# Where attention's blocks stand among the last projection slabs of a two-layer decoder trunk

## The chip, the core and the metric

The kernel runs on one core of a Trainium2 chip. The metric is device time in microseconds (us): the median of several runs of the whole program. The core has five engines that each run their own instructions in order and wait for each other through semaphores: TensorE (PE, matrix products), VectorE (DVE), ScalarE (ACT), GpSimd (POOL) and SyncE (SP, which here only issues transfers).

## What is computed

Two decoder layers over 512 tokens of width 1024. The first mixes with a causal convolution, the second with differential attention; each is followed by a gated feed-forward network and a gated per-layer embedding. The change concerns the attention of the second layer: 8 heads, each with two pairs of queries and keys of width 64 and values of width 128.

```python
qkv = x @ w_qkv
q, k, v = jnp.split(qkv, 3, axis=-1)
q = rms_norm(q.reshape(B, S, N_HEADS, 2, HEAD_DIM), q_g) * (HEAD_DIM ** -0.5)
k = rms_norm(k.reshape(B, S, N_HEADS, 2, HEAD_DIM), k_g)
...
def block(args):          # one block of 128 queries, all heads
    logits = jnp.einsum('bhcqd,bhckd->bhcqk', q_blk, k).astype(jnp.float32)
    logits = logits + bias[None, :, None]
    logits = jnp.where(dist >= 0, logits, -jnp.inf)
    probs = jax.nn.softmax(logits, axis=-1)
    w = probs[:, :, 0] - lam * probs[:, :, 1]
    return jnp.einsum('bhqk,bhkd->bhqd', w.astype(v.dtype), v)
...
o = rms_norm(o, sub_g) * (1.0 - lambda_init)
return o.reshape(B, S, N_HEADS * V_DIM) @ w_o
```

## The kernel before

Every fp32 product is made of three faster ones: a factor is split into a rounded part (`hi`) and the rest (`lo`), and `mm3` (lines 164 to 166) multiplies lo by hi, hi by lo and hi by hi. A weight tile arrives by DMA as `wraw`, ACT rounds it to `whi` (line 157), and DVE, for some tiles POOL, subtracts to get `wlo` (line 159).

**Slabs.** The projection to queries, keys and values is cut into seven slabs, listed in `QKV`. A slab of queries and keys (`"q"`, one pair of heads, 512 columns) takes four weight tiles; the values come as one full slab (`"v", (0, 4)`: heads 0 to 3, 512 columns) and two half slabs of 256 columns and two weight tiles each (heads 4 and 5, heads 6 and 7). Each slab is worked through in four units of 128 tokens (`tb` = 0 to 3), and a unit is 24 matmuls (8 chunks of the width, three products each) into a PSUM tile `mm`.

A unit of queries and keys (`unit`, then `unit_end`) is followed by a chain over the engines: ACT copies and squares (lines 909 and 912), DVE reduces (916), POOL takes the inverse root and scales (229 and 919), PE transposes (925), ACT and DVE write the split queries and keys (933, 934, 941, 943) and POOL copies (938). A unit of values only needs one row on ACT (892) and one on DVE (893).

**Blocks of attention.** Head `hd` and query block `qb` (0 to 3) make one block; its keys are the first 128 (qb + 1), so the four blocks of a head are 128, 256, 384 and 512 wide. A block has three stages. `stage_s`: PE makes the scores of both halves of a head into PSUM tiles `sc` (lines 970 and 971; tiles for up to 256 columns hold both halves), of which there are two; DVE adds the bias and takes the running minimum in one pass (973, called a reduction below), ACT takes the exponential (977), DVE combines both halves (980, 981, 982). `stage_t`: PE transposes the weights (990) into a tile `tp`, ACT and DVE split them (992, 993). `stage_a`: PE multiplies by the values (1006, 1007), and after each second block ACT and DVE collect the result (1013, 1014); after the fourth, lines 1018 to 1028 normalize the head. Blocks follow each other in order of head and query block; the scores of block n are written beside the transposes of block n - 2 and the products of block n - 3.

**What sets the order.** The stages of all blocks stand in one list. The third entry of each slab, its pace, says how many blocks each unit takes from it; a block is three entries, and they are written between the first matmuls of the unit:

```python
for what, at, pace in QKV:
    ws = slab(GLO if what == "q" and at > 0 else 0, P * at[1] if what == "v" else S)
    for tb in range(4):
        between = take(3 * pace[tb])
        between += [None] * (6 - len(between))
        ...
        if what == "v":
            values(at, ws, tb, between)
        else:
            waiting = unit(at, ws, tb, between)
```

What the slabs have not taken is spread over the projections that follow (`step`, inside `project` and the output projection). From the order in which the program is written a scheduler makes each engine's order of instructions; it may bring rows forward or back by a unit or so. The order is fixed in the program; the chip doesn't change it.

Of the kernel before, what the change touches and what calls it, by code (L numbers as in the profile page):

```python
# [64 lines left out]
for _c in range(NC):  # L65
    if _c in PHASED:
        TAPS += [(_c, g, m) for g in range(NPH) for m in (0, 4)] + [(_c, None, LAGS - 1)]
    else:
# [17 lines left out]
STEPS = (2, 2, 2, 3, 4, 5)  # L86
SEVEN = ((0,3),(1,0),(1,1),(1,2),(1,3),(2,0),(2,1),(2,2))
QKV = (("q", 0, (0, 0, 0, 0)), ("v", (0, 4), (0, 1, 1, 0)), ("q", 1, (1, 1, 2, 2)), ("q", 2, (0, 1, 2, 0)), 
       ("v", (4, 2), (1, 1, 1, 1)), ("q", 3, (0, 2, 0, 1)), ("v", (6, 2), (1, 1, 1, 1)))


@with_exitstack
# [1152 lines left out]
```

## Time and profile before

| | |
|---|---|
| median of 3 runs | 1267.42 us (1265.94 to 1268.10) |
| profiled execution | 1268.78 us; its span 1267.0 us |
| PE busy, share of the span | 1244.6 us, 98% |
| DVE busy | 903.4 us, 71% |
| ACT busy | 614.7 us, 49% |
| POOL busy | 263.3 us, 21% |
| mean granted clock of PE | 0.992 |

All times in the profile come from one execution, counted from the start of its span. The engines' busy times overlap, and a busy PE need not be working at its peak: matmuls are pipelined, so that the time from one start to the next is shorter than the duration shown. The granted clock is 1.00 when PE may run at full speed. In the rows of the trace, `out<-in` names the tiles without their numbers, and a bracket at the end gives the idle time of the engine just before the row and the instruction that ended it.

### The profile page before, as it was taken

Reading aid. Unit: us, or ns where it says so; the run is one execution under the profiler, and the core shown is the slowest. Engines: PE = TensorE matmul, PEld = TensorE weight load, DVE = VectorE, ACT = ScalarE, POOL = GpSimd, SP = SyncE. Lnnn points to the kernel's source line nnn. Section 1 sums busy time; section 2 is a strip of 40 time slices with the busy share of each in tenths; the row PEclk is TensorE's granted clock in tenths of the full one; section 3 lists DMA queues with packets and bytes.
Section 4 is the critical chain, followed back from the end, with each engine's and each line's share of the span. In section 5 each row is a group of like instructions: output and inputs, shape, how many; then the busy total and the mean of one; then the engine's idle time right before and its main releaser. Section 6 shows DMA issues by size and latency. Waiting matters only on the chain.

```text
span 1267.0 us, 18622 instructions
## 1 busy us (share of the span) xinstructions
PE 1244.6 (98%) x7152; PEld 1089.2 (86%) x7152; DVE 903.4 (71%) x1482; ACT 614.7 (49%) x1023; POOL 263.3 (21%) x231
## 2 busy tenths in 40 slices
PE   9999899999999999999999999999999999999998
PEld 7888678888899889988888978778898999899887
DVE  6997765975588558667678869845965588558665
ACT  6742464542355335456566757734542355235442
POOL 2852522000000000042516633122000000000030
PEclk9999999999999999999999989999999999999999
DMA  7665123474466444243222214213464467444241
GB/s 296 195 194 178 58 68 115 124 184 124 120 176 180 127 124 121 63 145 100 87 93 75 76 42 123 94 51 115 131 162 138 111 175 188 141 105 117 82 133 67
DMA packets 60597, 158.39 MB, mean 125 GB/s; under 512 B 6451, under 2 KB 11059, under 8 KB 60508
## 3 DMA queue, kind: packets, MB, share of 16 engines
q1 hardware_dynamic: 53776, 136.99, 34.3%
q0 software_dynamic: 4608, 16.78, 8.1%
q10 hardware_dynamic: 2124, 3.43, 0.9%
q8 instruction: 56, 0.92, 0.3%
q14 instruction: 33, 0.27, 0.1%
HBM read 151.91 MB, written 4.21 MB: 123 GB/s over the span
## 4 chain that ended last, share of the span: by engine, by line
PE 87%; DVE 6%; DMA 2%; ACT 2%; issue 1%; POOL 1%; SPq 0%; DVEq 0%; ACTq 0%; POOLq 0%
PE mm L164 24%; PE mm L165 24%; PE mm L166 24%; PE tp L166 2%; PE tp L165 2%; PE tp L164 2%; PE sc L165 1%; PE sc L166 1%; PE sc L164 1%; DVE wlo L159 1%; POOL wk L409 1%; DMA po<-big 1%; PE sc L370 1%; PE mm L1006 1%; DVE sc L421 1%
## 5 line engine op out<-in xcount | busy, mean ns | idle before, releaser
L165 PE MATMUL mm<-A,whi 128*128 128x512 f32 (+1 forms) x904 | 311.8, 346 | 1.0 <-DVE A L569 0.7
L164 PE MATMUL mm<-A,wlo 128*128 128x512 f32 (+1 forms) x904 | 308.0, 345 | 3.5 <-ACT A L178 1.8
L166 PE MATMUL mm<-A,whi 128*128 128x512 f32 (+1 forms) x904 | 310.2, 344 | 0.0
L157 ACT CAST whi<-wraw 128x1024 fp32r<-128x1024 f32 (+2 forms) x150 | 151.1, 1015 | 224.5 <-PE mm L166 98.5
L159 DVE TENSOR_TENSOR wlo<-wraw,whi 128x1024 fp32r<-128x1024 f32 (+2 forms) x147 | 185.1, 1262 | 58.4 <-ACT whi L157 58.1
L164 PEld LDWEIGHTS mm<-A,wlo 128*128 128x128 f32 x904 | 171.4, 190 | 25.0 <-ACT A L178 2.7
L165 PEld LDWEIGHTS mm<-A,whi 128*128 128x128 f32 x904 | 171.9, 190 | 22.1 <-issue 1.2
L166 PEld LDWEIGHTS mm<-A,whi 128*128 128x128 f32 x904 | 171.9, 190 | 21.0 <-issue 1.4
L165 PE MATMUL mm<-B,whi 128*128 128x512 f32 x368 | 143.9, 392 | 0.0
L166 PE MATMUL mm<-B,whi 128*128 128x512 f32 x368 | 143.8, 392 | 0.0
L164 PE MATMUL mm<-B,wlo 128*128 128x512 f32 x368 | 141.6, 393 | 0.0
L675 POOL DMA_DIRECT2D C<-in_wts x32 | 28.1, 880 | 511.8 <-DVE h L786 179.0
L204 POOL TENSOR_TENSOR acc<-acc,wk 128x512 f32<-128x512 f32 x35 | 56.4, 1610 | 218.1 <-ACT wk L203 110.7
L166 PEld LDWEIGHTS mm<-B,whi 128*128 128x128 f32 x368 | 69.5, 189 | 15.0
L166 PE MATMUL mm<-whi,A 128*128 128x512 f32 (+1 forms) x224 | 82.0, 367 | 0.0
L164 PEld LDWEIGHTS mm<-B,wlo 128*128 128x128 f32 x368 | 69.5, 189 | 14.3
L165 PEld LDWEIGHTS mm<-B,whi 128*128 128x128 f32 x368 | 69.4, 189 | 14.3
L165 PE MATMUL mm<-wlo,A 128*128 128x512 f32 (+1 forms) x224 | 81.6, 367 | 0.0
L164 PE MATMUL mm<-whi,A 128*128 128x512 f32 (+1 forms) x224 | 81.6, 370 | 0.0
L786 DVE TENSOR_TENSOR h<-mm,h 128x512 f32<-128x512 f32 x48 | 33.0, 687 | 64.6 <-PE mm L166 64.4
L229 POOL TENSOR_TENSOR r<-v,mhalf 128x8 f32<-128x8 f32 (+1 forms) x31 | 45.4, 1465 | 118.4 <-DVE v L227 93.1
L668 DVE TENSOR_TENSOR wlo<-wraw,whi 128x1024 fp32r<-128x1024 f32 x32 | 39.2, 1224 | 31.5 <-ACT whi L667 31.4
(271 smaller groups left out, 2674.2 us busy)
## 6 DMA issues: line engine op xcount, KB each, us to landing
wraw<-in_wts SPq DMA_DIRECT2D x162, 512.0 KB, 3.6
C<-in_wts SPq DMA_DIRECT2D x32, 512.0 KB, 4.8
C<-in_wts POOLq DMA_DIRECT2D x32, 512.0 KB, 6.1
bias<-in_wts SPq DMA_DIRECT2D x32, 256.0 KB, 3.4
wraw<-in_wts SPq DMA_DIRECT2D x16, 384.0 KB, 3.1
D<-in_diag SPq DMA_DIRECT2D x22, 256.0 KB, 4.5
C<-in_diag SPq DMA_DIRECT2D x16, 256.0 KB, 4.7
h<-in_xT SPq DMA_DIRECT2D x8, 256.0 KB, 5.5
```

Source lines behind the costliest of these rows:

```text
L157: A.copy(hi[:, cut], raw[:, cut])
L159: eng.tensor_tensor(lo[:, cut], raw[:, cut], f(hi[:, cut]), ALU.subtract)
L164: T.matmul(acc, al, bh, start=first, stop=False)
L165: T.matmul(acc, ah, bl, start=False, stop=False)
L166: return T.matmul(acc, ah, bh, start=False, stop=last)
L204: self.last = self.eng.tensor_tensor(self.acc, self.acc, sq, ALU.add)
L229: last_pow[0] = G.tensor_tensor(r[:, :n], v[:, :n], mhalf[:, :n], ALU.pow)
L370: last_tap[0] = T.matmul(acc[:, g * P : (g + 1) * P], w, ups[c][:, g, LEAD - m : LEAD - m + P], start=(m == 0), stop=(m == LAGS - 1),)
L409: G.tensor_tensor(pacc, pacc, pr, ALU.add)
L668: V.tensor_tensor(lo, raw, f(hi), ALU.subtract)
L675: nc.gpsimd.dma_start(q, wts[i + 2].rearrange("p (a s) -> p a s", a=2), accum_op=ALU.add)
L786: V.tensor_tensor(h[m], acc, h[m], ALU.add)
```

## The change

One table of numbers is changed: the paces of the last three slabs. In blocks per unit:

| slab | before | now |
|---|---|---|
| values of heads 4 and 5 (half slab) | 1, 1, 1, 1 | 0, 1, 0, 1 |
| queries and keys of heads 6 and 7 | 0, 2, 0, 1 | 1, 2, 1, 2 |
| values of heads 6 and 7 (half slab) | 1, 1, 1, 1 | 1, 1, 1, 0 |

```diff
 QKV = (("q", 0, (0, 0, 0, 0)), ("v", (0, 4), (0, 1, 1, 0)), ("q", 1, (1, 1, 2, 2)), ("q", 2, (0, 1, 2, 0)), 
-       ("v", (4, 2), (1, 1, 1, 1)), ("q", 3, (0, 2, 0, 1)), ("v", (6, 2), (1, 1, 1, 1)))
+       ("v", (4, 2), (0, 1, 0, 1)), ("q", 3, (1, 2, 1, 2)), ("v", (6, 2), (1, 1, 1, 0)))
```

Both tables take eleven blocks in these three slabs, so that the tail begins with the same block. The list's first entries are shorter (the first blocks have no transposes or products beside them), so the scores are a little ahead of the count. Before, the first half slab wrote the scores of head 3's blocks 1, 2, 3 and head 4's block 0, the slab of queries and keys those of head 4's blocks 1, 2, 3, and the last half slab all four of head 5. Now the first half slab writes head 3's blocks 1 and 2, the slab of queries and keys head 3's block 3, all of head 4 and head 5's block 0, and the last half slab head 5's blocks 1, 2 and 3.

In the rows below a name is a tile with its number; `sc` are scores, `mm` sums of a slab or of the products with the values, `tp` transposes, `C` split queries and keys, `B` values, `A` the normalized input of the projections. Numbers of tiles differ between the programs.

PE, at the end of the half slab of heads 4 and 5, before. `sc_6955` is the second half of head 3's 512-wide block, `sc_7005` is head 4's block 0:

```order
L970 MATMUL sc_6955<-C_1095_6055,C_1093_6053 128x512
L971 MATMUL sc_6955<-C_1097_6057,C_1093_6053 128x512
L990 MATMUL tp_6894<-ident_65,big_6672 128x128
L1007 MATMUL mm_6866<-B_1051_5867,wtl_6826 128x128
L1006 MATMUL mm_6866<-B_1065_5941,wth_6825 128x256
L1007 MATMUL mm_6866<-B_1065_5941,wtl_6826 128x128
L1006 MATMUL mm_6866<-B_1077_5997,wth_6825 128x256
L1007 MATMUL mm_6866<-B_1077_5997,wtl_6826 128x128
L1006 MATMUL mm_6866<-B_1079_6025,wth_6825 128x256
L1007 MATMUL mm_6866<-B_1079_6025,wtl_6826 128x128
L970 MATMUL sc_7005<-C_1191_6465,C_1189_6463 128x128
L971 MATMUL sc_7005<-C_1193_6467,C_1189_6463 128x128
```

Only eight small rows stand between the scores of head 3's last block and those of head 4; the scores of head 4's block 1 (`sc_7130`) come next, and then the slab of queries and keys begins.

PE at the same place now, from the first row of the slab of queries and keys (`mm_7006`) on; `sc_7037` and `sc_7043` are head 3's 512-wide block:

```order
L164 MATMUL mm_7006<-whi_6975,A_928_5273 128x512
L165 MATMUL mm_7006<-wlo_6976,A_927_5272 128x512
L166 MATMUL mm_7006<-whi_6975,A_927_5272 128x512
L990 MATMUL tp_6863<-ident_65,big_6635 128x128 x4
L164 MATMUL mm_7006<-whi_6975,A_931_5283 128x512
L165 MATMUL mm_7006<-wlo_6976,A_930_5282 128x512
L166 MATMUL mm_7006<-whi_6975,A_930_5282 128x512
L970 MATMUL sc_7037<-C_1094_6054,C_1092_6052 128x512
L971 MATMUL sc_7037<-C_1096_6056,C_1092_6052 128x512
L970 MATMUL sc_7043<-C_1095_6055,C_1093_6053 128x512
L971 MATMUL sc_7043<-C_1097_6057,C_1093_6053 128x512
L164 MATMUL mm_7006<-whi_6981,A_939_5326 128x512
```

The scores of head 3's last block now stand behind six matmuls of the next slab, and more of them follow at once; head 4's scores come some thirty rows later.

DVE at the same place, before, from the first value split behind the reductions of head 3's 384-wide block:

```order
L893 SCALAR_TENSOR_TENSOR B_1291_6989<-mm_6918,rcol_5628,B_1291_6989 128x2x128
L993 TENSOR_TENSOR wtl_6826<-tp_6820,wth_6825 128x512
L981 SCALAR_TENSOR_TENSOR st_6668<-st_6668,lam_5564 128x1
L973 ISA big_6952,st_6668<-sc_6949,bias_6666 128x512
L973 ISA st_6668 128x1
L980 RECIPROCAL st_6668<-st_6668 128x1
L982 SCALAR_TENSOR_TENSOR big_6806<-rb_6811,st_6668,big_6806 128x256
L159 TENSOR_TENSOR wlo_7062<-wraw_7060,whi_7061 128x1024
L981 SCALAR_TENSOR_TENSOR st_6668<-st_6668,lam_5564 128x1
L893 SCALAR_TENSOR_TENSOR B_1302_7045<-mm_6992,rcol_5628,B_1302_7045 128x2x128
L973 ISA rb_6958,st_6668<-sc_6955,bias_6666 128x512
L973 ISA st_6668 128x1
```

The two 512-wide reductions stand among rows of the 384-wide block and behind a weight split (line 159).

DVE now, from the weight split behind the same 384-wide reductions:

```order
L159 TENSOR_TENSOR wlo_6988<-wraw_6986,whi_6987 128x1024
L980 RECIPROCAL st_6668<-st_6668 128x1
L981 SCALAR_TENSOR_TENSOR st_6668<-st_6668,lam_5564 128x1
L982 SCALAR_TENSOR_TENSOR big_6935<-acc_6941,st_6668,big_6935 128x384
L941 SCALAR_TENSOR_TENSOR C_1189_6463<-tp_6811,lam_5564,C_1189_6463 64x2x128
L943 SCALAR_TENSOR_TENSOR C_1193_6467<-tp_6811,vec_63,C_1191_6465 64x2x128
L941 SCALAR_TENSOR_TENSOR C_1190_6464<-tp_6811,lam_5564,C_1190_6464 64x2x128
L943 SCALAR_TENSOR_TENSOR C_1194_6468<-tp_6811,vec_63,C_1192_6466 64x2x128
L893 SCALAR_TENSOR_TENSOR B_1281_6971<-mm_6918,rcol_5628,B_1281_6971 128x2x128
L973 ISA big_7040,st_6668<-sc_7037,bias_6666 128x512
L973 ISA st_6668 128x1
L973 ISA rb_7046,st_6668<-sc_7043,bias_6666 128x512
```

The two 512-wide reductions (results `big_6952` and `rb_6958`, now `big_7040` and `rb_7046`) have moved from among the 384-wide block's rows to behind the last rows of the unit of queries and keys (`tp_6811`) and the last value split (`B_1281`), and no reduction of head 4 stands near.

DVE where head 5's scores are first reduced, before (`sc_7408` is its block 0):

```order
L159 TENSOR_TENSOR wlo_7375<-wraw_7373,whi_7374 128x1024
L227 TENSOR_SCALAR v_1354_7271<-v_1353_7269 128x8
L941 SCALAR_TENSOR_TENSOR C_1315_7072<-tp_7247,lam_5564,C_1315_7072 64x2x128
L943 SCALAR_TENSOR_TENSOR C_1319_7076<-tp_7247,vec_63,C_1317_7074 64x2x128
L941 SCALAR_TENSOR_TENSOR C_1316_7073<-tp_7247,lam_5564,C_1316_7073 64x2x128
L943 SCALAR_TENSOR_TENSOR C_1320_7077<-tp_7247,vec_63,C_1318_7075 64x2x128
L1020 TENSOR_REDUCE v_1358_7292<-wk_7290 128x4
L159 TENSOR_TENSOR wlo_7381<-wraw_7379,whi_7380 128x1024
L980 RECIPROCAL st_7004<-st_7004 128x1
L973 ISA big_7411,st_7407<-sc_7408,bias_7405 128x128
```

Four rows of lines 941 and 943 and a line 1020 stand between the two weight splits.

DVE at that place now (`sc_7344` is head 5's block 0):

```order
L159 TENSOR_TENSOR wlo_7403<-wraw_7401,whi_7402 128x1024
L227 TENSOR_SCALAR v_1354_7271<-v_1353_7269 128x8
L159 TENSOR_TENSOR wlo_7409<-wraw_7407,whi_7408 128x1024
L973 ISA big_7347,st_7343<-sc_7344,bias_7341 128x128
L973 ISA st_7343 128x1
L980 RECIPROCAL st_7100<-st_7100 128x1
L1020 TENSOR_REDUCE v_1358_7292<-wk_7290 128x4
L981 SCALAR_TENSOR_TENSOR st_7100<-st_7100,lam_5564 128x1
L941 SCALAR_TENSOR_TENSOR C_1294_6998<-tp_7247,lam_5564,C_1294_6998 64x2x128
L943 SCALAR_TENSOR_TENSOR C_1298_7002<-tp_7247,vec_63,C_1296_7000 64x2x128
L941 SCALAR_TENSOR_TENSOR C_1295_6999<-tp_7247,lam_5564,C_1295_6999 64x2x128
L943 SCALAR_TENSOR_TENSOR C_1299_7003<-tp_7247,vec_63,C_1297_7001 64x2x128
```

The two weight splits (line 159) stand next to each other ahead of the reduction, and the four rows of lines 941 and 943 on `tp` of the third unit, which stood ahead of it, stand behind.

## The prediction

> **What bounds the kernel now.** I read the page first, then the stretch that the change touches by windows, then the waits of TensorE (PE) and VectorE (DVE) there, and last single rows in order of time.
>
> ```profile
> PE 1244.6 (98%) x7152; PEld 1089.2 (86%) x7152; DVE 903.4 (71%) x1482; ACT 614.7 (49%) x1023; POOL 263.3 (21%) x231
> PE 87%; DVE 6%; DMA 2%; ACT 2%; issue 1%; POOL 1%; SPq 0%; DVEq 0%; ACTq 0%; POOLq 0%
> ```
>
> The first line is the share of busy time, the second the chain that ended last. PE bounds the kernel as a whole, so a change can only win where PE stands still or runs slowly. The change touches the time from about 715 to 800 us; these windows cut it at the places where its character changes (columns: PE, weight loads, DVE, ACT, POOL busy, then the granted clock, DMA share, GB/s). The first row and the last lie outside the change and serve for comparison.
>
> ```profile
> 680.00:683.50 3.50, 1.90 (x11) 1.39 (x10) 3.46 (x11) 1.68 (x5) 3.32 (x3) 1.00 0.25 44
> 715.75:728.40 12.65, 12.65 (x103) 12.36 (x102) 12.23 (x34) 9.25 (x25) 8.81 (x9) 1.00 0.29 84
> 728.40:731.60 3.20, 1.67 (x12) 1.17 (x10) 3.20 (x9) 3.20 (x7) 0.95 (x1) 1.00 0.00 0
> 731.60:738.40 6.80, 5.93 (x16) 4.72 (x17) 6.66 (x21) 4.43 (x14) 1.89 (x2) 0.50 0.63 193
> 738.40:764.70 26.30, 26.30 (x140) 22.35 (x139) 14.97 (x46) 14.96 (x34) 9.95 (x11) 1.00 0.04 10
> 764.70:782.40 17.70, 17.65 (x140) 16.77 (x138) 17.02 (x48) 13.87 (x34) 8.54 (x10) 1.00 0.48 135
> 782.40:786.30 3.90, 1.90 (x14) 1.64 (x14) 3.83 (x8) 3.58 (x10) 0.00 (x0) 1.00 0.18 74
> 786.30:789.70 3.40, 3.40 (x11) 2.73 (x10) 3.33 (x11) 1.85 (x6) 0.00 (x0) 0.50 0.57 159
> 789.70:798.20 8.50, 6.92 (x44) 4.96 (x42) 7.39 (x26) 6.46 (x18) 0.98 (x1) 1.00 0.49 155
> 840.40:846.00 5.60, 3.83 (x15) 2.85 (x16) 4.62 (x7) 3.73 (x6) 0.75 (x1) 1.00 0.01 3
> ```
>
> The reader is to see three stages. To 738.4, in the half slab of heads 4 and 5, DVE works without a pause and PE runs dry: it idles 1.53 + 0.87 = 2.40 us, and then its clock stands at 0.50 for 6.80 us, which is worth another 3.40 us. From 738.4 to 764.7, in the slab of the last queries and keys, PE is full and DVE idles 26.30 - 14.97 = 11.33 us. From 764.7 to 798.2, in the half slab of heads 6 and 7 and behind it, DVE is full again and PE idles 0.05 + 2.00 + 0.00 + 1.58 = 3.63 us and loses 1.70 us to the clock. All that PE loses from 715.75 to 798.20 is 2.40 + 3.40 + 3.63 + 1.70 = 11.1 us. The waits between 715 and 800 us say the same: PE waits for DVE, and DVE waits only for PE's results.
>
> ```profile
> PE sc L970 <- DVE st L973: 2.4, 2, 2.1
> PE tp L990 <- DVE C L943: 1.7, 1, 1.7
> DVE C L941 <- ACT C L934: 4.8, 2, 4.4
> DVE big L973 <- PE tp L990: 3.4, 1, 3.4
> ```
>
> The first of these is the hole before the loss of the clock. In order of time:
>
> ```profile
> 724.00 0.55 DVE L973 CUSTOM_DVE_ANT_0 big<-sc,bias 128x384 f32<-128x384 f32 x1
> 727.40 0.56 DVE L973 CUSTOM_DVE_ANT_0 acc<-sc,bias 128x384 f32<-128x384 f32 x1
> 730.07 1.22 DVE L159 TENSOR_TENSOR wlo<-wraw,whi 128x1024 fp32r<-128x1024 f32 x1
> 731.73 0.68 DVE L973 CUSTOM_DVE_ANT_0 rb<-sc,bias 128x512 f32<-128x512 f32 x1
> 730.11 0.27 PE L971 MATMUL sc<-C,C 128*128 128x128 f32 x1
> 732.47 0.58 PE L970 MATMUL sc<-C,C 128*128 128x256 f32 x1 [2.09 <-DVE st L973]
> ```
>
> PE has two score tiles (sc). After 730.11 its next row in program order is a score pair for head 4, and it may not write until DVE has reduced the last tile of head 3, which starts at 731.73, behind a weight split (L159). The matmuls of the next slab stand behind that score pair in PE's order and wait with it.
>
> **The change, part by part.** No instruction is added or removed: PE, DVE, ACT, POOL and SP issue as many rows as before, with the same shapes. What moves is the last block of head 3 and the first block of head 4 (out of the half slab of heads 4 and 5 into the slab of queries and keys) and the first block of head 5 (out of the half slab of heads 6 and 7 into that same slab). In SP's queue the loads keep their order; ACT's queue issues the bias of heads 4, 5 and 6 between other rows, which costs nothing as long as DVE reads a bias much later than it is issued, as it does.
>
> *The first hole, -5.8 us.* In the new order the half slab holds only the 256- and 384-wide blocks of head 3. The 512-wide score tiles come six slab matmuls into the next slab, and the two tiles that they take over are those whose reductions start at 724.00 and 727.40 now (in the new order one short value split, L893, comes ahead of the second). When does PE get there?
>
> ```profile
> 727.60 0.28 PE L1006 MATMUL mm<-B,wth 128*128 128x256 f32 x1
> 739.31 0.39 PE L166 MATMUL mm<-whi,A 128*128 128x512 f32 x1
> 739.54 0.40 PE L164 MATMUL mm<-whi,A 128*128 128x512 f32 x1
> 758.80 0.60 PE L925 MATMUL tp<-ident,big 128*128 128x128 f32 x4
> 759.15 0.47 PE L971 MATMUL sc<-C,C 128*128 128x512 f32 x1
> ```
>
> Matmuls overlap, so what one costs is the time from its start to the next start: 0.23 us for 512 columns, 0.35 for four transposes. The half slab is over at 727.60 now; two 512-wide score matmuls and four transposes (0.8 us) have left it, and six slab matmuls and four transposes (1.7 us) come ahead of the scores: 727.6 - 0.8 + 1.7 = 728.5, and both tiles are free. So the wait of 2.09 us, with what surrounds it (2.40), goes, and without a stop of that length I also take the loss of the clock (3.40) as gone. What is late next on DVE is the split of the third weight tile, which PE needs only after another eleven slab matmuls.
>
> *The slab of queries and keys, 0 us.* It takes in three blocks. The cover is DVE's 11.33 idle us. One 512-wide block costs DVE two reductions, one combination and one split of the transposed weights, the 128-wide ones less:
>
> ```profile
> L973 DVE CUSTOM_DVE_ANT_0 big<-sc,bias 128x512 f32<-128x512 f32 x4 | 2.7, 675 | 0.0
> L982 DVE SCALAR_TENSOR_TENSOR big<-rb,st,big 128x512 f32<-128x512 f32 x4 | 3.0, 746 | 0.0
> L993 DVE TENSOR_TENSOR wtl<-tp,wth 128x512 fp32r<-128x512 f32 x4 | 2.7, 683 | 0.0
> L973 DVE CUSTOM_DVE_ANT_0 acc<-sc,bias 128x128 f32<-128x128 f32 x4 | 1.1, 282 | 0.0
> L941 DVE SCALAR_TENSOR_TENSOR C<-tp,lam,C 64x256 fp32r<-64x256 f32 x14 | 6.8, 484 | 5.0 <-ACT C L934 4.8
> L1020 DVE TENSOR_REDUCE v<-wk 128x4 f32<-128x512 f32 x3 | 2.0, 683 | 0.0
> L993 DVE TENSOR_TENSOR wtl<-tp,wth 128x384 fp32r<-128x384 f32 x4 | 2.2, 552 | 0.0
> L980 DVE RECIPROCAL st<-st 128x1 f32<-128x1 f32 x14 | 2.2, 157 | 1.0 <-ACT rb L977 0.9
> ```
>
> The large block is 2 x 0.68 + 0.75 + 0.68 = 2.8 us, the two small ones at most half of that each: some 5.6 us, half of the cover. If the cover were gone, PE would stop here as it did at 730, and that is a rival below.
>
> *The last stretch.* I compare two marks on DVE: the first reduction of head 5, and the point in head 6 where its second 384-wide tile and its first 512-wide tile are both reduced, after which the two programs run almost the same rows.
>
> ```profile
> 764.72 0.23 PE L970 MATMUL sc<-C,C 128*128 128x128 f32 x1
> 765.18 0.28 PE L165 MATMUL mm<-wlo,A 128*128 128x256 f32 x1
> 765.29 0.28 PE L166 MATMUL mm<-whi,A 128*128 128x256 f32 x1
> 767.70 0.29 DVE L973 CUSTOM_DVE_ANT_0 big<-sc,bias 128x128 f32<-128x128 f32 x1
> 799.04 0.54 DVE L973 CUSTOM_DVE_ANT_0 acc<-sc,bias 128x384 f32<-128x384 f32 x1
> ```
>
> PE issues the first scores of head 5 at 764.72 now. In the changed order six transposes (0.09 us each), two 256-wide slab matmuls (0.11 each) and one small matmul less stand ahead: 0.8 us. With the first hole gone PE is there at 764.72 - 5.8 - 0.8 = 758.1. DVE reduced it 3.0 us late, at 767.70, since it was behind by then. In the changed order it has been idle more recently, but two weight splits of 1.2 us stand just ahead; between 0.2 (straight after) and 3.0 I take 1.0: DVE is there at 759.1, which is 8.6 earlier than 767.70. From this mark on DVE is the bound, and it has more to do than before, since more rows have come to stand behind the mark: two more groups of L941 with its twin L943 (4 x 0.48 = 1.9), one more L1020 (0.68) and two tiny ones (L980 and its like, 0.3), against one 384-wide split less (0.55): 2.3 us more. The bounds are 0.4, if they fill the 33.50 - 31.57 = 1.9 us that DVE idles in the windows from 764.70 to 798.20, and 2.9 without the split. So the lead at the second mark is 8.6 - 2.3 = 6.3 us.
>
> *Behind it, 0 us.* The tail has the same rows in nearly the same order, and PE is full there. The stop of 840.40 to 846.00 stays.
>
> *The clock in the last stretch, 0 us* against before, which lost one spell of 1.70 there. DVE stays the bound for 34 us, and PE has as much to do as before, so it will stop about as much. The rows give no sharp rule: the stop at 730 cost 6.80 us at half clock, the one at 782.4 cost 3.40, but those at 680 (1.60 us idle) and 840 (1.77 us idle) cost nothing. So bounds are 1.70 less and 3.4 more.
>
> On this the Trainium skill (TensorE: Matmul & The Clock Gate, Part 1) says that the clock falls to half after an idle window of about 3.4 us and comes back after a busy one. The lengths of the two spells, 3.40 and twice that, agree; the condition does not, since here a stop of 2.09 us was enough. By the page's condition no stop in the new order would be long enough, the bounds of this term would be 1.70 less and 0, and the second and third rival below would lose the 3.4 us that they rest on.
>
> *The sum:* -5.8 - 0.8 - (3.0 - 1.0) + 2.3 = -6.3 us. The profiled execution took 1268.78 us (span 1267.0), 1.4 above the median of the runs, 1267.42; it would become 1262.5, and the median 1261.1.
>
> **The rivals.** *More is won:* the 2.3 us of extra DVE rows vanish in the waits that DVE had, as PE is ahead of it. The lead of 8.6 then holds: 1258.8; if every loss from 715.75 to 798.20 went, 1267.42 - 11.1 = 1256.3. For it speaks that DVE's work is the same in sum and better spread; against it that DVE is full from the second mark on in both.
>
> *Nothing is seen:* DVE still comes 3.0 us late to head 5 (+2.0), and PE's stops, now closer together between the two marks, cost two more spells at half clock (+3.4): -6.3 + 5.4 = -0.9, 1266.5. For it speaks that PE must idle more densely there, as it arrives early; against it that PE at half clock costs nothing while DVE is the one that is late.
>
> *Slower:* the hole moves into the slab of queries and keys. There ACT and DVE run in order through the reductions of head 4 and the unit's own steps (L909, L912, L916), each waiting for PE; if DVE hangs behind such a row as it did for 4.4 us on L934, PE meets a score pair whose tile is not free. It decides from a stop of about 2 us on, since from there the clock goes: 2.40 + 3.40 back, and with the second rival's 3.4 it is -6.3 + 5.8 + 3.4 = +2.9: 1270.3. Against it speaks the cover of 11.33 against 5.6 us.
>
> **How the numbers follow.** The forecast has 0.58, more is won 0.15, nothing seen 0.16, slower 0.11. A change of 0.2% (2.5 us) is about what can be told from none. Faster takes the first two and a little of the third: 0.74; same 0.15; slower 0.11. The range leaves out most of the slower case and the farthest of the gain: 1256.8 to 1266.8.
>
> **What would show it.** Right: no clock below 1.00 between 720 and 745 us and no wait of PE on a score tile there; DVE idle in the slab of queries and keys about 5 instead of 11 us; the first 128-wide reduction of head 5 near 759; DVE full from there to about 793. Wrong: a wait of 2 us on L970 before 755 (third rival), more than one spell of half clock between 765 and 795 with PE's project matmuls inside it (second), or PE free of waits there (first).

## The result, and the profile after

The changed kernel took 1261.22 us in the median (1260.06 to 1261.39), the kernel before beside it 1267.76 us; the ratio is 0.9949 (0.9936 to 0.9962). A second comparison gave 1261.52 against 1265.94 us, ratio 0.9966 (0.9955 to 0.9978). So the change is worth 4.3 to 6.5 us by the two ratios and 2.8 to 8.1 us by their intervals; the forecast was 6.3.

The page of the changed kernel shows little of it (first the busy times, then the chain that ended last):

```profile
PE 1240.0 (98%) x7152; PEld 1087.0 (86%) x7152; DVE 904.7 (72%) x1482; ACT 615.1 (49%) x1023; POOL 263.0 (21%) x231
PE 91%; DVE 4%; DMA 2%; ACT 1%; POOL 1%; issue 1%; SPq 0%; DVEq 0%; ACTq 0%; POOLq 0%
```

PE's busy time fell by 4.6 us with the same rows, since fewer of them ran at half clock; DVE's part of the chain fell from 6 to 4%. The windows of the changed kernel, with the same columns as before:

```profile
715.00:728.00 13.00, 13.00 (x97) 12.29 (x96) 12.52 (x35) 9.72 (x27) 7.95 (x9) 1.00 0.19 66
727.00:751.00 24.00, 24.00 (x134) 20.75 (x133) 18.53 (x56) 14.22 (x38) 10.72 (x11) 1.00 0.19 56
751.00:772.00 21.00, 21.00 (x158) 20.03 (x157) 20.65 (x55) 18.67 (x43) 10.20 (x12) 1.00 0.27 88
772.00:788.00 16.00, 12.09 (x62) 9.60 (x62) 15.21 (x44) 12.22 (x30) 0.79 (x2) 0.89 0.51 148
788.00:797.00 9.00, 8.39 (x52) 6.77 (x51) 8.70 (x29) 7.76 (x21) 2.05 (x2) 1.00 0.41 142
```

From 715 to 772 us PE has no idle time and no half clock: the hole at 730 us and its 6.80 us at half clock are gone, and in the slab of queries and keys DVE idles 24.00 - 18.53 = 5.5 us instead of 11.3. From 772 us on PE stops as before, and once the clock falls. The stops, in order of time, are waits for DVE and for ACT:

```profile
773.90 0.50 PE L970 MATMUL sc<-C,C 128*128 128x512 f32 x1 [0.90 <-DVE st L973]
776.85 0.38 PE L1006 MATMUL mm<-B,wth 128*128 128x256 f32 x1 [0.97 <-ACT wth L992]
782.25 0.38 PE L1006 MATMUL mm<-B,wth 128*128 128x256 f32 x1 [1.05 <-ACT wth L992]
783.09 0.38 PE L970 MATMUL sc<-C,C 128*128 128x256 f32 x1 [0.46 <-DVE st L973]
784.11 1.06 PE L1035 MATMUL tp<-ident,D 128*128 128x128 f32 x4 [0.52 <-DVE wtl L993]
```

To compare the two executions row by row, one needs a common start, since what happens ahead of the change differs too. Two stops that both programs have, at 680 and 845 us in the kernel before, bound the stretch that the change can move. First the two rows of before, then those of the changed kernel:

```profile
682.48 0.30 PE L970 MATMUL sc<-C,C 128*128 128x128 f32 x1 [1.60 <-DVE st L973]
845.20 0.50 PE L164 MATMUL mm<-A,wlo 128*128 128x512 f32 x1 [1.74 <-DVE wlo L159]
```

```profile
679.98 0.30 PE L970 MATMUL sc<-C,C 128*128 128x128 f32 x1 [1.61 <-DVE st L973]
837.70 0.50 PE L164 MATMUL mm<-A,wlo 128*128 128x512 f32 x1 [1.75 <-DVE wlo L159]
```

The stretch took 845.20 - 682.48 = 162.72 us before and 837.70 - 679.98 = 157.72 us after: 5.0 us. The other 2.5 us by which the spans differ (1267.0 and 1259.5) lie ahead of the change. There the clock happened to fall once more in the execution of before, which explains at most 1.7 of them:

```profile
8.00:11.40 3.40, 3.40 (x9) 2.63 (x9) 3.40 (x6) 3.35 (x7) 0.00 (x0) 0.50 1.07 400
```

The changed kernel's marks for the sum are these rows, on PE the first scores of head 5, on DVE their reduction, and the later of the two reductions of the second mark:

```profile
755.40 0.22 PE L970 MATMUL sc<-C,C 128*128 128x128 f32 x1
757.74 0.29 DVE L973 CUSTOM_DVE_ANT_0 big<-sc,bias 128x128 f32<-128x128 f32 x1
790.69 0.69 DVE L973 CUSTOM_DVE_ANT_0 big<-sc,bias 128x512 f32<-128x512 f32 x1
```

### The profile page after: what moved, and what is told of

It reads as the page before. It is cut to its first block, busy times and chain, and to the rows that moved or that the text cites. A ratio compares the mean times of both kernels' runs of the same rounds, so it can differ in the third digit from the quotient of the medians.

```text
span 1259.5 us, 18626 instructions
## 1 busy us (share of the span) xinstructions
PE 1240.0 (98%) x7152; PEld 1087.0 (86%) x7152; DVE 904.7 (72%) x1482; ACT 615.1 (49%) x1023; POOL 263.0 (21%) x231
## 4 chain that ended last, share of the span: by engine, by line
PE 91%; DVE 4%; DMA 2%; ACT 1%; POOL 1%; issue 1%; SPq 0%; DVEq 0%; ACTq 0%; POOLq 0%
PE mm L164 25%; PE mm L165 25%; PE mm L166 24%; PE tp L166 2%; PE tp L165 2%; PE tp L164 2%; PE sc L165 1%; PE sc L166 1%; PE sc L164 1%; PE mm L1006 1%; POOL wk L409 1%; DMA po<-big 1%; PE sc L370 1%; PE sc L970 1%; PE sc L971 1%
```

## The experiments

"The stretch" below is the time between those two stops in one profiled execution. Comparisons are over five rounds, that of the kernel before with itself over three.

**Both kernels again.** No edit.

> The changed kernel once more, beside the others of this comparison: about 6 us less than before (4.8 to 8.1 by its first runs). Its profile gives a second look at PE's stops in the last stretch (4.6 us from 772 to 797 us in the first profile) and at whether the spell of half clock there comes back.

> The kernel before once more, for a second profiled execution. In the first one the stretch from PE's stop at 680 us to the end of its stop at 845 us took 162.7 us, against 157.7 and 157.4 in the two executions of the changed kernel, and 2.5 us of the difference of the two first spans lay ahead of that stretch. Theory (the 5.0 us are the change, the 2.5 chance): the stretch takes 161 to 163 us again with two spells of half clock behind 730 us, and the part ahead of it is about 2 us shorter than in the first. Rival (the loss of the clock at 730 us is itself chance): no such spell this time, and a stretch of 158 to 160 us.

The changed kernel: ratio 0.9966 (0.9955 to 0.9978), 4.3 us less than before where 6 were expected; stretch 157.43 us, the same stops as in the first profile within 0.2 us, one spell of half clock again. The kernel before: ratio 1.0006 (0.9995 to 1.0016), stretch 161.06 us. The hole at 730 us and 6.8 us of half clock behind it came back as they were:

```profile
729.97 0.58 PE L970 MATMUL sc<-C,C 128*128 128x256 f32 x1 [2.09 <-DVE st L973]
```

The spell in the last stretch did not come back, although PE stopped there again for 1.67 us. So the loss at 730 us belongs to the program (the two other programs below that keep the hole lose the same 6.8 us), the one of 1.7 us near 786 us to the single execution, and the stretch gains 3.3 to 5.3 us.

**The first half of the change alone.**

```diff
-("v", (4, 2), (1, 1, 1, 1)), ("q", 3, (0, 2, 0, 1)), ("v", (6, 2), (1, 1, 1, 1))
+("v", (4, 2), (0, 1, 0, 1)), ("q", 3, (1, 2, 1, 1)), ("v", (6, 2), (1, 1, 1, 1))
```

> Paces (0,1,0,1), (1,2,1,1), (1,1,1,1): the half slab of heads 4 and 5 is thinned as in the change, but all four blocks of head 5 stay in the last half slab. Theory (the gain is the first hole and its clock): no half clock between 720 and 745 us, PE waits under 0.5 us there, and 5.8 us less than before (5 to 7), the last stretch losing about what it lost before (3.6 us of stops, one spell of 3.4 us at half clock). Rival (the first block of head 5 has to move too, since otherwise the last half slab gives back what the first has won): 3 us less than before or nothing.

Ratio 0.9978 (0.9966 to 0.9990), 2.8 us less than before by the ratio and 2.2 by the medians; the stretch took 158.8 us. The hole is gone, and head 5's first reduction comes as early as in the change (77.82 us from the start of the stretch against 77.76). But in the last half slab, which here has all four blocks of head 5, PE now stops longer than in either kernel, and the clock falls for two spells:

```profile
776.61 0.33 PE L970 MATMUL sc<-C,C 128*128 128x128 f32 x1 [1.55 <-DVE st L973]
778.98 0.45 PE L990 MATMUL tp<-ident,big 128*128 128x128 f32 x1 [1.26 <-DVE C L943]
780.50 0.58 PE L1006 MATMUL mm<-B,wth 128*128 128x256 f32 x1 [1.08 <-ACT wth L992]
778.60:785.40 6.80, 5.35 (x13) 4.12 (x14) 6.26 (x14) 3.57 (x9) 0.00 (x0) 0.50 0.35 107
```

The rival was right: what the first half wins is partly given back, unless the last half slab is thinned too.

**The second half alone.**

```diff
-("q", 3, (0, 2, 0, 1)), ("v", (6, 2), (1, 1, 1, 1))
+("q", 3, (0, 2, 0, 2)), ("v", (6, 2), (1, 1, 1, 0))
```

> Paces (1,1,1,1), (0,2,0,2), (1,1,1,0): only the first block of head 5 moves into the slab of queries and keys, the first half slab is left as before. Theory: the hole at 730 us (2.1 us of wait and 6.8 us at half clock) stays, and the time is that of before within 1 us. Rival (thinning the last half slab is worth what it takes from DVE there, 2 to 3 us): 2.5 us less than before.

Ratio 1.0015 (0.9995 to 1.0035), stretch 164.5 us. The hole stayed, and nothing was won behind it: PE stops there for 2.5 us in one piece, at 775 us, and the last stretch has two spells of half clock. The two halves add up to less (2.8 us and nothing) than the whole (4.3 to 6.5).

**More of the same.** One more block of head 5, and two more:

```diff
-("q", 3, (1, 2, 1, 2)), ("v", (6, 2), (1, 1, 1, 0))
+("q", 3, (1, 2, 2, 2)), ("v", (6, 2), (1, 0, 1, 0))
```

```diff
-("q", 3, (1, 2, 1, 2)), ("v", (6, 2), (1, 1, 1, 0))
+("q", 3, (2, 2, 2, 2)), ("v", (6, 2), (0, 1, 0, 0))
```

> Paces (0,1,0,1), (1,2,2,2), (1,0,1,0): one more block than in the change, the 256-wide one of head 5, moves from the last half slab into the slab of queries and keys. It costs DVE about 1.8 us, and DVE still idles 5.3 us there (732 to 751 us) in the changed kernel. Theory (DVE's load in the last stretch is what PE waits for, and the slab before has room): 1 to 2 us less than the changed kernel, PE's stops from 772 to 797 us falling from 4.6 to about 3. Rival (the last stretch is bound by the chains of its blocks, or the cover is gone): no gain, within 0.6 us of the changed kernel.

> Paces (0,1,0,1), (2,2,2,2), (0,1,0,0): eight blocks in the slab of queries and keys, the 384-wide one of head 5 as well. Some 4.1 us of DVE work against 5.3 idle us. Theory: 2 to 4 us less than the changed kernel. Rival (the cover is gone, the hole comes back inside the slab of queries and keys): a wait of PE on a score tile of 1 us or more between 735 and 760 us, and a time not below that of six blocks.

Both theories failed: ratios 1.0005 (0.9991 to 1.0019) and 1.0001 (0.9992 to 1.0010), so by the medians all of the gain is lost (the one profile with eight blocks has a stretch of 160.2 us, that with seven 163.6). For seven blocks it is worse than the rival had it, too. With seven blocks PE runs on to 761 us without a stop, but the slab's own chain is pushed back. These are the transposes of its third and fourth unit (L925), first in the changed kernel, then with seven blocks, where a stop of PE follows:

```profile
763.02 0.60 PE L925 MATMUL tp<-ident,big 128*128 128x128 f32 x4
772.41 0.60 PE L925 MATMUL tp<-ident,big 128*128 128x128 f32 x4
```

```profile
772.63 0.60 PE L925 MATMUL tp<-ident,big 128*128 128x128 f32 x4
780.01 0.60 PE L925 MATMUL tp<-ident,big 128*128 128x128 f32 x4
786.92 1.94 PE L1035 MATMUL tp<-ident,D 128*128 128x128 f32 x8 [2.63 <-DVE C L943]
```

From the start of the stretch they come 9.4 and 7.3 us later, the rows of lines 941 and 943 on them as well, and PE waits 2.63 us for the last of those; another stop, of 1.92 us, stands just ahead. The delay of the third unit is already there in DVE's reduction of it (L916), again first in the changed kernel, then with seven blocks, 9.4 us later from the start of the stretch; ACT's square ahead of it (L912) comes 4.1 us later:

```profile
754.48 0.68 DVE L916 TENSOR_REDUCE v<-wk 128x8 f32<-128x512 f32 x1
764.09 0.68 DVE L916 TENSOR_REDUCE v<-wk 128x8 f32<-128x512 f32 x1
```

With eight blocks PE stops for DVE at once (0.73 us at 733 us, less than the rival asked for), and in the last stretch for 2.5 us in one piece. DVE's idle 5.5 us were no room for them: on DVE and ACT the blocks' rows came ahead of the slab's own chain.

**One block less.**

```diff
-("v", (6, 2), (1, 1, 1, 0))
+("v", (6, 2), (1, 1, 0, 0))
```

> Paces (0,1,0,1), (1,2,1,2), (1,1,0,0): as in the change, but the last block of head 5 (512 wide, some 2.8 us of DVE work) is left to the projections that follow, so the three slabs take ten blocks instead of eleven. Theory (DVE has more work than time in the last half slab, and what it takes over later costs the same there, since the output projection waits for all heads): within 1 us of the changed kernel, PE's stops moving from 772 to 785 us to behind it. Rival (the place counts: the reductions and splits of the last unit of queries and keys come earlier, head 6 starts sooner): 1 to 2 us less.

Ratio 0.9952 (0.9940 to 0.9963), median 1260.58, stretch 156.64 us: 0.8 to 1.1 us less in the stretch than the changed kernel, which the medians (0.9 us) cannot tell from nothing.

**DVE's split ahead of the hole.** The kernel before, with one weight tile of the slab subtracted by POOL:

```diff
-ws = [weight(eng=G if i < n else V) for i in range(NC // per)]
+ws = [weight(eng=G if i in n else V) for i in range(NC // per)]
...
-ws = slab(GLO if what == "q" and at > 0 else 0, P * at[1] if what == "v" else S)
+ws = slab(((0,) if at < 3 else (0, 2)) if what == "q" and at > 0 else (), P * at[1] if what == "v" else S)
```

> The kernel before, its paces untouched, with the third weight tile of the last slab of queries and keys subtracted by POOL instead of DVE: the row of 1.22 us that stands ahead of the reduction PE waits for at 730 us. Theory (DVE is late there by its own rows, and the loss of the clock hangs on how long PE stops): the wait of 2.09 us falls to about 0.9; if the clock then stays, 1.2 + 3.4 = 4.6 us less than before, if it falls anyway, 1.2 us less. Rival (only the place of the blocks decides, as other DVE rows take the split's place): nothing, within 0.6 us.

Ratio 1.0019 (1.0003 to 1.0034), slower, and PE's stop grew from 2.09 to 3.59 us. A tiny row of DVE tells why. First DVE and POOL in this run, then the same DVE row in the kernel before:

```profile
727.75 2.31 DVE L981 SCALAR_TENSOR_TENSOR st<-st,lam 128x1 f32<-128x1 f32 x1
727.51 2.53 POOL L159 TENSOR_TENSOR wlo<-wraw,whi 128x1024 fp32r<-128x1024 f32 x1 [2.84 <-issue]
731.64 0.58 PE L970 MATMUL sc<-C,C 128*128 128x256 f32 x1 [3.59 <-DVE st L973]
```

```profile
731.21 0.21 DVE L981 SCALAR_TENSOR_TENSOR st<-st,lam 128x1 f32<-128x1 f32 x1
```

The row on 128x1 took 2.31 instead of 0.21 us and ended when POOL's subtraction did. DVE waited for POOL, longer than the split on DVE would have taken (1.22). The account closes: 1.1 us less for the split, 2.1 more for this row and 0.5 for a combination (L982) that also came ahead of the reduction make 1.5 us, as the stop grew. What the run was to decide, it did not decide. The Trainium skill (SBUF — State Buffer, "Who interferes with whom") says that a VectorE instruction with two inputs in SBUF contends with a GpSimd instruction that reads SBUF, for ports that are an exclusive lock; this run agrees, with 2.31 us.

**Three splits of the last stretch on POOL.** The changed kernel, the second tile of the projection and the first two of the output projection:

```diff
-            w = weight()
+            w = weight(eng=G if m else V)
...
-            ws = [weight(n_in * P, after=first[i] if m == 0 else None) for i in range(g)]
+            ws = [weight(n_in * P, after=first[i] if m == 0 else None, eng=G if after and m == 0 else V) for i in range(g)]
```

> The changed kernel, with three weight tiles (the second of the projection behind the last half slab, the first two of the output projection) subtracted by POOL instead of DVE. Theory (DVE is the bound from 751 to about 790 us in the changed kernel): 3 x 1.2 us less for DVE there; of PE's stops from 773 to 784 us (3.9 us) at least 2 go, and with them perhaps the spell of 3.4 us at half clock (1.7 us): 2 to 4.5 us less than the changed kernel, about 8 to 11 less than before. Rival (PE waits there for ACT's rounding and for the chain of a block, not for DVE's load, or POOL's subtraction of 2.4 us comes late): the time of the changed kernel within 1 us.

Ratio 0.9963 (0.9944 to 0.9983), the time of the changed kernel. Here too a row of line 981 stretched, to 1.57 us at 779.60 beside a subtraction on POOL from 778.75 to 781.16, so the run leaves open what less work on DVE would be worth. The next one does not.

**The same three splits left out.** `few` is 64 for the three tiles and 0 for all others.

```diff
+few and G.memset(f(lo[:, few:]), 0.0)
-eng.tensor_tensor(lo[:, cut], raw[:, cut], f(hi[:, cut]), ALU.subtract)
+eng.tensor_tensor(lo[:, cut][:, : few or None], raw[:, cut][:, : few or None], f(hi[:, cut])[:, : few or None], ALU.subtract)
```

> The changed kernel, which subtracts only 64 of 1024 columns of the three weight tiles that went to POOL in the run above (the rest of the lower parts is set to zero by POOL, so the products with them are left out in substance): 3 x 1.15 us less for DVE in the last stretch, without a subtraction on POOL that DVE could wait for. Theory (DVE's load is what PE waits for from 772 to 797 us): of PE's 4.6 us of stops there at least 2.5 go, 2.5 to 5 us less than the changed kernel. Rival (PE waits for single chains, split after exponential after reduction, whatever DVE's load): under 1 us less.

Ratio 0.9960 (0.9945 to 0.9974), stretch 157.93 us, against 157.72 and 157.43 of the changed kernel. DVE does get ahead: head 7's first reduction comes 110.86 us behind the start of the stretch, 4.0 earlier than in the changed kernel (114.90). DVE's busy time between 88 and 127 us of the stretch falls from 36.6 to 33.9 us, 2.7 instead of the 3.4 planned: one of the three shortened splits took 1.07 instead of 0.22 us, beside a row of POOL. PE's stops only move; in the same 39 us they sum to 5.1 us against 4.7. The two largest, from the trace of this run (it is 11 us later at that place, mostly because PE ran at half clock for 20.5 us near 150 us, ahead of the stretch):

```profile
787.50 0.38 PE L970 MATMUL sc<-C,C 128*128 128x256 f32 x1 [1.20 <-DVE st L973]
798.62 0.66 PE L1035 MATMUL tp<-ident,D 128*128 128x128 f32 x4 [1.48 <-DVE A L179]
```

The rival was right: in the last stretch PE waits for single rows in the order in which they stand, not for the sum of DVE's work.

**Work for PE in the hole.** The kernel before, with matmuls without use:

```diff
+[T.matmul(both, qs[c][:, i, cut], u[0][0], start=True, stop=True) for _ in range(9 * ((hd, qb, c) == (4, 0, 0)))]
 T.matmul(acc[:, :n], qs[c][:, i, cut], ks[c][:, i, 0:n], start=True, stop=False)
```

> The kernel before with nine more matmuls of 512 columns, written into the score tile of head 4's first block ahead of its scores and overwritten by them: 9 x 0.23 = 2.1 us of work without use, at the place where PE waits 2.09 us at 730 us. Theory (the clock falls because PE idles in one stretch of 3.4 us): PE's wait there falls under 0.4 us and no half clock follows, the matmuls of the slab behind run at full pace, and head 5 is reached 3.4 us earlier; of that the last stretch may give back up to 3, as it did where only the first half slab was thinned, so 0.4 to 3.4 us less than before. Rival (the clock falls for another reason, such as the load of the engines together): half clock from 731 us on as before, and the time of before plus up to 1 us.

The nine rows filled the hole, and the clock stayed up, 1.00 in the window behind it:

```profile
727.61 2.29 PE L970 MATMUL sc<-A,C 128*128 128x512 f32 x9
731.00:738.00 7.00, 6.74 (x32) 5.62 (x33) 5.80 (x16) 2.96 (x9) 1.93 (x2) 1.00 0.49 154
```

So the half clock at this place comes from PE's own idleness. Head 5's first scores were reached 2.1 us earlier than before, not 3.4 as the theory had it: before, the slab's matmuls ran at half clock only from 734.03 to 738.48 us, which is worth 2.2, while the rest of the spell fell on the stop and on small rows. The stretch took 159.7 us against 161.1 and 162.7, with stops of 1.66 and 0.85 us and a spell of half clock at 781 us. In the medians only 1.3 us are left, and the ratio, 0.9992 (0.9982 to 1.0002), does not tell that from nothing. The mean granted clock over all executions of this comparison was 0.9960 against 0.9955 before. A spell of 6.83 us is worth 0.0027, so by this estimate most of what was kept here was lost again elsewhere in these executions.

**Work for PE in the last stretch.** The same edit in the changed kernel, four matmuls each ahead of head 6's blocks 0 and 1.

> The changed kernel with four matmuls of 512 columns without use ahead of the first scores of head 6's blocks 0 and 1 (8 x 0.23 = 1.8 us, overwritten by the scores), where PE idles 0.98 and 1.06 us in the profile. Theory (the clock falls where PE idles too much within one stretch of 3.41 us, on a grid that lies differently in each execution): these two stops shrink to 0.1 each, the spell of half clock between 775 and 800 us goes, 1 to 1.7 us less than the changed kernel. Rival (the extra work only pushes the chain behind it back, and the clock falls anyway): 0 to 1.8 us more.

Ratio 0.9967 (0.9955 to 0.9978). In the profile no half clock appeared between 690 and 1250 us, the stop of 0.97 us at 777 us went, that of 1.05 us at 782 us shrank to 0.24, and another grew from 0.52 to 1.04; the stretch took 156.95 us, 0.5 to 0.8 less than the changed kernel, and the median is that of the changed kernel. The mean granted clock over all executions is 0.9978, against 0.9973 of the changed kernel in its second comparison, where one spell is worth 0.0014; so the spell did not go in all executions. What a lost spell costs here stays open: 0.8 us at most by these profiles, while in the kernel before the one that came and went near 786 us made 1.7.

## Why the prediction was right, step by step

In times from the start of the stretch, so that what lies ahead does not count:

| mark | before | changed | earlier by | forecast |
|---|---|---|---|---|
| PE, first scores of head 5 | 82.24 | 75.42 | 6.8 | 5.8 + 0.8 = 6.6 |
| DVE, their reduction | 85.22 | 77.76 | 7.5 | 8.6 |
| DVE, second mark | 116.56 | 110.71 | 5.9 | 6.3 |
| end of the stretch | 162.72 | 157.72 | 5.0 | 6.3 |

The second profiles of both kernels give 6.8, 7.4, 4.5 and 3.6 us earlier in these four rows.

- *The first hole, -5.8:* right in mechanism. The stops of 2.40 us and the 6.80 us at half clock are gone, and the run with work for PE in the hole shows that the clock hung on the stop. The two terms of the size overlap: 0.87 of the 2.40 us of idle time lie inside the 6.80 us, so by the same rows the clock cost PE at most (6.80 - 0.87) / 2 = 2.97 us, and the hole 5.4.
- *The rows ahead of head 5's scores, -0.8:* PE's rows between the two marks bear it out: six transposes, two 256-wide slab matmuls and two small rows fewer. With 5.4 it makes 6.2 of the 6.8 us; where the other 0.6 come from stays open.
- *The slab of queries and keys, 0:* right for six blocks, PE never waits there. The reason given, DVE's idle time as cover, was incomplete: two more blocks fitted into that idle time by the sum of their rows, and cost the whole gain.
- *DVE's lateness at head 5, 3.0 to 1.0:* mis-sized. DVE came 77.76 - 75.42 = 2.3 us late. The two weight splits that stand ahead of the reduction (2 x 1.14) are the whole of it; the forecast let them count for less than one.
- *Extra DVE rows behind the mark, +2.3:* 7.5 - 5.9 = 1.6, inside the bounds of 0.4 to 2.9; 7.4 - 4.5 = 2.9 in the second profiles, where before has no spell in this part.
- *Behind it, 0:* 0.9 us were given back there, in both pairs of profiles. At the second mark the changed kernel has 44 matmuls of 512 columns of each of the lines 164 to 166 ahead of it in the stretch, the kernel before 43: three matmuls, 0.7 us. The mark on DVE did not show that PE was less far.
- *"From this mark on DVE is the bound":* wrong as a cause. It was full, but 2.7 us less work on it changed nothing in the time.
- *The clock in the last stretch, 0:* one spell in the first profiles of both, none in the second of before. A matter of chance from run to run, inside the bounds that were named. Over all executions of the second comparison the mean granted clock rose from 0.9955 to 0.9973; 0.0018 of 1265 us are 2.3 us. By this estimate some 1.1 of the 3.4 us that the forecast had for the clock came back elsewhere.

The errors of 1.4 (lateness), -0.7 (rows), 0.9 (behind) and -0.2 (up to head 5's scores) sum to 1.3 us with the rounding, so that profile against profile the stretch gave 5.0 of the 6.3 us. That the medians of the first comparison differ by 6.5 us, nearly the forecast, is luck of the executions that stood beside each other; the second gave 4.4.

Of the rivals, "slower" did not come with this change. Its mechanism shows in part when more is moved: with eight blocks PE stops on a score tile in the slab, with seven only behind it, for the slab's own chain. "Nothing is seen" lived in the first half alone: PE arrived early and met a denser row of stops with two spells of half clock.

## What to carry to other kernels

Moving work from a stage where a helper engine is full to one where it idles pays where the wait that ends last is the one removed, and only as far as the moved rows don't push the receiving stage's own chain back: sum the idle time, but also ask which rows come behind the moved ones in each queue, and who waits for those. Thinning one full stage sends the work on earlier into the next full one, so judge the two together. Compare traces from a common row onward, and profile the kernel before twice, since a spell of half clock that one execution has and the next has not is as large as such a change's terms.

## What the runs showed of the hardware

The clock is judged on a fixed grid of 3.413 us. In the first profile of before, spells of half clock begin at 154.80, 731.65 and 786.26 us, 169 and 16 such steps apart, and in all fourteen profiled executions every change of the clock behind 100 us and ahead of the end lies whole steps from the others; a spell lasts one or two steps (six once, at 146 us in the run with the three splits left out). The place of the grid differs from execution to execution: the next point of it comes 0.3 to 2.9 us behind the end of the stop at 680 us.

Counted behind 100 us, each of the 21 grid steps at full clock in which PE idled 1.84 us or more was followed by half clock, and none in which it idled less than 1.3 us; of the 34 between these, 9 were. So a stop of 1.85 us near 152 us, which all programs have, was followed by half clock in the nine executions in which it lay within one step, and not in the four in which it lay across a point of the grid (in the fourteenth the clock was already down from a longer stop ahead of it). The stop of 1.6 us at 680 us, which lies among full matmuls, cost the clock in none. The Trainium skill (TensorE: Matmul & The Clock Gate, Part 1) describes such a free-running window and asks for an idle one; the length and the free run agree with these traces, but half a window of idleness was enough.

POOL's subtraction of a weight tile stopped a tiny DVE row for 2.31 us, another one for 1.57 us, and a subtraction of 64 columns on DVE took 1.07 instead of 0.22 us beside POOL's scaling of a unit (line 919): work moved to an idle POOL is not free for DVE.
